# A FiLM layer on one core: x kept whole in SBUF as four slabs, longer transfer runs, small loads on another queue, rows split between VectorE and GpSimd

## The chip, the cores and the metric

One NeuronCore of a Trainium2 chip. The metric is device microseconds of that core, lower is better. Each figure is the median of a kernel's fast runs; runs of the kernel before, taken on the same chip in the same rounds, stand beside each. An execution counts as slow when it takes over 1.5% more than the fastest of the same kernel; slow ones are left out.

Names in the profiles: PE is TensorE (matmul), PEld its weight load, DVE VectorE, ACT ScalarE, POOL GpSimd, SP SyncE; a q behind a name stands for that engine's queue, with its waits and DMA issues. L100 is line 100 of the kernel. The profile counts 16 DMA engines for the core. A run is a stretch of contiguous bytes of one partition, and in the traces here each run of x or of the output is one packet (before: 4096 packets of 8 KB; after: 128 of 8, 1024 of 16, 128 of 24 and 384 of 32 KB). "Before" is the kernel before, "after" the changed one.

## The reference

```python
gamma = conditioning @ gamma_proj          # (32, 64) @ (64, 256)
beta = conditioning @ beta_proj
return x * (1 + gamma[:, None, :]) + beta[:, None, :]    # x: (32, 512, 256) float32
```

x is 16.8 MB, the output is as large, and all else is 0.14 MB.

## The kernel before

Two batch entries (1 MB) make a tile of 128 partitions with 8 rows of 256 in each. A small matmul spreads gamma and beta of the two entries over the partitions, into PSUM. VectorE does `(gamma + 1) * x` and `+ beta` in place. SyncE issues all loads, ScalarE all stores, 12 tiles are in flight.

```python
nc.sync.dma_start(out=cond_s, in_=conditioning)
nc.sync.dma_start(out=gbproj[:, :dim], in_=gamma_proj)
nc.sync.dma_start(out=gbproj[:, dim:], in_=beta_proj)
# ... cond_T, gb_s (32 x 512), one-hot matrix rident ...
for bg in range(0, batch, 2):                                   # 16 turns
    nc.sync.dma_start(out=x_tile, in_=...)                      # 1 MB, 8 KB per partition
    nc.tensor.matmul(gbbc, lhsT=onehot, rhs=gb_s, ...)          # 128 x 512 into PSUM
    nc.vector.scalar_tensor_tensor(out=x_tile, in0=gbc_k, scalar=1.0, in1=x_tile, op0=add, op1=mult)
    nc.vector.tensor_add(out=x_tile, in0=x_tile, in1=bbc_k)
    nc.scalar.dma_start(out=..., in_=x_tile)                    # 1 MB, 8 KB per partition
```

Of the kernel before, what the change touches and what calls it, by code (L numbers as in the profile page):

```python
# [2 lines left out]

# [5 lines left out]


@with_exitstack
def kernel(
    ctx: ExitStack,
    tc: tile.TileContext,
    x: bass.AP,
    conditioning: bass.AP,
    gamma_proj: bass.AP,
    beta_proj: bass.AP,
    out: bass.AP,  # L20
):
    nc = tc.nc
    f32 = mybir.dt.float32

    batch, seq, dim = x.shape
    cond_dim = conditioning.shape[1]
    assert conditioning.shape == (batch, cond_dim)
    assert gamma_proj.shape == (cond_dim, dim)
    assert beta_proj.shape == (cond_dim, dim)
    assert batch <= 128 and cond_dim <= 128  # L30

    P = 128
    assert seq % P == 0
    K = seq // P

    x_flat = x.flatten_outer_dims()
    out_flat = out.flatten_outer_dims()

    consts = ctx.enter_context(tc.tile_pool(name="consts", bufs=1))
    work = ctx.enter_context(tc.tile_pool(name="work", bufs=12))  # L40
    psum = ctx.enter_context(tc.tile_pool(name="psum", bufs=6, space=bass.MemoryType.PSUM))

    def x_src(b):
        r0 = b * seq
        return x_flat[r0 : r0 + seq, :].rearrange("(p k) d -> p k d", p=P)

    def out_dst(b):
        r0 = b * seq
        return out_flat[r0 : r0 + seq, :].rearrange("(p k) d -> p k d", p=P)

    cond_s = consts.tile([batch, cond_dim], f32)
    nc.sync.dma_start(out=cond_s, in_=conditioning)  # L52

    gbproj = consts.tile([cond_dim, 2 * dim], f32)
    nc.sync.dma_start(out=gbproj[:, :dim], in_=gamma_proj)  # L55
    nc.sync.dma_start(out=gbproj[:, dim:], in_=beta_proj)

    ident = consts.tile([P, P], f32)
    make_identity(nc, ident)

    with tc.tile_pool(name="psum0", bufs=1, space=bass.MemoryType.PSUM) as psum0:
        cond_T_p = psum0.tile([cond_dim, batch], f32)
        nc.tensor.matmul(cond_T_p, lhsT=cond_s, rhs=ident[:batch, :batch],  # L63
                         start=True, stop=True)
        cond_T = consts.tile([cond_dim, batch], f32)
        nc.vector.tensor_copy(out=cond_T, in_=cond_T_p)  # L66

        gb_p = psum0.tile([batch, 2 * dim], f32)
        nc.tensor.matmul(gb_p, lhsT=cond_T, rhs=gbproj, start=True, stop=True)  # L69
        gb_s = consts.tile([batch, 2 * dim], f32)  # L70
        nc.vector.tensor_copy(out=gb_s, in_=gb_p)  # L71

    BG = 2
    assert batch % BG == 0 and P % BG == 0
    PG = P // BG
    KK = (BG * seq) // P
    assert PG * KK == seq

    rident = consts.tile([batch, batch * PG], f32)
    nc.vector.tensor_copy(  # L80
        out=rident.rearrange("p (b g) -> p b g", g=PG),
        in_=ident[:batch, :batch].to_broadcast([batch, batch, PG]),
    )

    for bg in range(0, batch, BG):
        x_tile = work.tile([P, KK, dim], f32, name="x_tile")
        r0 = bg * seq
        nc.sync.dma_start(  # L88
            out=x_tile,
            in_=x_flat[r0 : r0 + BG * seq, :].rearrange("(p k) d -> p k d", p=P),  # L90
        )

        onehot = rident[:batch, bg * PG : bg * PG + P]
        gbbc = psum.tile([P, 2 * dim], f32)
        nc.tensor.matmul(gbbc, lhsT=onehot, rhs=gb_s, start=True, stop=True)  # L95

        gbc = gbbc[:, :dim]
        bbc = gbbc[:, dim:]
        gbc_k = bass.AP(tensor=gbc.tensor, offset=gbc.offset,
                        ap=[gbc.ap[0], [0, KK], gbc.ap[1]])  # L100
        bbc_k = bass.AP(tensor=bbc.tensor, offset=bbc.offset,
                        ap=[bbc.ap[0], [0, KK], bbc.ap[1]])

        nc.vector.scalar_tensor_tensor(  # L104
            out=x_tile,
            in0=gbc_k,
            scalar=1.0,
            in1=x_tile,
            op0=mybir.AluOpType.add,
            op1=mybir.AluOpType.mult,  # L110
        )
        nc.vector.tensor_add(out=x_tile, in0=x_tile, in1=bbc_k)  # L112

        nc.scalar.dma_start(
            out=out_flat[r0 : r0 + BG * seq, :].rearrange("(p k) d -> p k d", p=P),
            in_=x_tile,
        )


# [1 line left out]
_INS = ['x', 'conditioning', 'gamma_proj', 'beta_proj']  # L121
_OUTS = [((32, 512, 256), 'float32')]


# [23 lines left out]
```

## Time and profile before

| | before |
|---|---|
| time | 87.56 us (87.53 to 87.76) |
| span of the profiled execution | 85.5 us |
| moved by DMA | 33.70 MB, 4816 packets |
| VectorE busy | 72.5 us, 85% |
| GpSimd busy | 0.7 us |

The span runs from the first instruction to the last. In every run of this study but e6 the time is about 1.8 us more than its span (87.57 with 85.8, 84.35 with 82.6). A profile is one execution: the one shown here, with 85.5 us, is one of the faster ones. The prediction shows the strip of the transfers, the stretches, VectorE's two groups and the start; one view it left out is how long the small loads took from issue to landing (name, queue, how many, KB each, us):

```profile
gbproj<-in_gamma_proj_dram SPq DMA_DIRECT2D x1, 64.0 KB, 2.1
gbproj<-in_beta_proj_dram SPq DMA_DIRECT2D x1, 64.0 KB, 2.2
cond_s<-in_conditioning_dram SPq DMA_DIRECT2D x1, 8.0 KB, 1.5
```

Issued first, with nothing else to move, each lands within some 2 us. That will change.

### The profile page before, as it was taken

The page shows a single profiled execution, that of the slowest core. Times are in us where ns is not written, and L with a number is a line of the kernel's source. Part 1 is how long each engine was busy: PE and PEld are TensorE (multiplying, and loading weights), DVE is VectorE, ACT ScalarE, POOL GpSimd, SP SyncE. Part 2 cuts the span into 40 slices and gives each one's busy share as a digit, 9 for nine tenths or more (in the row PEclk, how much of TensorE's full clock was granted, in tenths as well). Part 3 has the DMA queues.
Part 4 walks back from the last instruction along what each step waited for, and adds up shares of the span by engine and source line. Part 5 has one row for each costly group of instructions (what it writes and reads, how often), then busy time and mean ns, then how long its engine had stood idle before and what let it go on. Part 6 is the DMA issues. An engine that isn't in the chain of part 4 may idle for free.

```text
span 85.5 us, 241 instructions
## 1 busy us (share of the span) xinstructions
PE 32.6 (38%) x36; PEld 9.6 (11%) x36; DVE 72.5 (85%) x35; POOL 0.7 (1%) x6
## 2 busy tenths in 40 slices
PE   0288999997059404950396019700000000000000
PEld 0203434340022002200220022000000000000000
DVE  3211899999999999999999999999999999999000
POOL 3000000000000000000000000000000000000000
DMA  0689999999999999999999999999999999999991
GB/s 4 123 368 418 425 429 425 429 330 356 429 429 425 429 429 429 429 429 425 429 425 429 429 429 429 418 429 429 429 425 429 429 425 429 418 429 422 429 429 58
DMA packets 4816, 33.70 MB, mean 394 GB/s; under 512 B 592, under 2 KB 720, under 8 KB 720
## 3 DMA queue, kind: packets, MB, share of 16 engines
q1 hardware_dynamic: 2512, 16.92, 48.9%
q10 hardware_dynamic: 2304, 16.78, 46.4%
HBM read 16.92 MB, written 16.78 MB: 394 GB/s over the span
## 4 chain that ended last, share of the span: by engine, by line
DMA 43%; DVE 32%; issue 9%; PE 5%; DVEq 3%; SPq 1%
DMA x_tile<-in_x_dram 28%; DVE x_tile L104 20%; DMA out_dram<-x_tile 12%; DVE x_tile L112 11%; DMA gbproj<-in_beta_proj_dram 3%; DVEq L143 3%; PE gbbc L95 2%; PE gb_p L69 2%; DVE gb_s L71 1%; SPq L55 1%; SPq L52 0%; SPq L88 0%; DVEq L104 0%
## 5 line engine op out<-in xcount | busy, mean ns | idle before, releaser
L104 DVE SCALAR_TENSOR_TENSOR x_tile<-gbbc,x_tile 128x2048 f32<-128x2048 f32 x16 | 35.9, 2283 | 2.2 <-PE gbbc L95 2.2
L95 PE MATMUL gbbc<-gb_s,rident 32*128 32x512 f32 x32 | 30.3, 1094 | 18.8 <-DVE x_tile L112 18.0
L112 DVE TENSOR_TENSOR x_tile<-x_tile,gbbc 128x2048 f32<-128x2048 f32 x16 | 35.8, 2279 | 0.0
L95 PEld LDWEIGHTS gbbc<-gb_s,rident 32*128 32x128 f32 x32 | 9.1, 317 | 40.2 <-issue 30.8
L71 DVE COPY gb_s<-gb_p 32x512 f32<-32x512 f32 x1 | 0.7, 679 | 3.1 <-PE gb_p L69 3.1
L69 PE MATMUL gb_p<-gbproj,cond_T 64*32 64x512 f32 x2 | 1.9, 1042 | 1.4 <-DMA gbproj<-in_beta_proj_dram 1.4
L80 DVE COPY rident<-ident 32x2048 f32<-32x2048 f32 x1 | 1.2, 1214 | 1.3 <-POOL ident masks.py:199 1.3
L63 PE MATMUL cond_T_p<-ident,cond_s 32*64 32x32 f32 x2 | 0.4, 284 | 2.4 <-DMA cond_s<-in_conditioning_dram 2.4
L63 PEld LDWEIGHTS cond_T_p<-ident,cond_s 32*64 32x64 f32 x2 | 0.3, 202 | 2.4 <-issue 2.4
L66 DVE COPY cond_T<-cond_T_p 64x32 f32<-64x32 f32 x1 | 0.2, 183 | 0.3 <-PE cond_T_p L63 0.3
L69 PEld LDWEIGHTS gb_p<-gbproj,cond_T 64*32 64x32 f32 x2 | 0.2, 132 | 1.5 <-issue 1.5
masks.py:199 POOL TENSOR_SCALAR_AFFINE_SELECT ident<-ident 128x128 f32<-128x128 f32 x1 | 0.3, 294 | 0.1
masks.py:197 POOL MEMSET ident<- 128x128 f32 x1 | 0.2, 205 | 0.3 <-POOLq L132 0.3
L132 POOL MEMSET const-bfloat16-1.0<- 128x1 bf16 x1 | 0.1, 102 | 0.0
L132 POOL MEMSET const-uint8-127<- 128x1 uint8 x1 | 0.1, 102 | 0.0
L132 POOL MEMSET const-float32-0.0<- 128x1 f32 x1 | 0.1, 99 | 0.2 <-issue 0.2
L132 POOL MEMSET const-float32-1.0<- 128x1 f32 x1 | 0.1, 99 | 0.0
## 6 DMA issues: line engine op xcount, KB each, us to landing
x_tile<-in_x_dram SPq DMA_DIRECT2D x16, 1024.0 KB, 20.5
out_dram<-x_tile ACTq DMA_DIRECT2D x16, 1024.0 KB, 12.4
gbproj<-in_gamma_proj_dram SPq DMA_DIRECT2D x1, 64.0 KB, 2.1
gbproj<-in_beta_proj_dram SPq DMA_DIRECT2D x1, 64.0 KB, 2.2
cond_s<-in_conditioning_dram SPq DMA_DIRECT2D x1, 8.0 KB, 1.5
```

What stands on the lines that cost most here:

```text
L55: nc.sync.dma_start(out=gbproj[:, :dim], in_=gamma_proj)
L63: nc.tensor.matmul(cond_T_p, lhsT=cond_s, rhs=ident[:batch, :batch], start=True, stop=True)
L66: nc.vector.tensor_copy(out=cond_T, in_=cond_T_p)
L69: nc.tensor.matmul(gb_p, lhsT=cond_T, rhs=gbproj, start=True, stop=True)
L71: nc.vector.tensor_copy(out=gb_s, in_=gb_p)
L80: nc.vector.tensor_copy(out=rident.rearrange("p (b g) -> p b g", g=PG), in_=ident[:batch, :batch].to_broadcast([batch, batch, PG]),)
L95: nc.tensor.matmul(gbbc, lhsT=onehot, rhs=gb_s, start=True, stop=True)
L104: nc.vector.scalar_tensor_tensor(out=x_tile, in0=gbc_k, scalar=1.0, in1=x_tile, op0=mybir.AluOpType.add, op1=mybir.AluOpType.mult,)
L112: nc.vector.tensor_add(out=x_tile, in0=x_tile, in1=bbc_k)
L132: nc = _bacc.Bacc("TRN2", target_bir_lowering=False, num_devices=1)
L143: with _tile.TileContext(nc) as tc:
```

## The change

The intent: all of x fits into SBUF (4 slabs of 32 KB per partition, 128 KB together, which the changed kernel holds), so no load ever has to wait for a buffer; the runs per partition grow from 8 KB to 32 KB (loads) and 16 KB (stores); x is issued at once while ScalarE's queue takes the small loads; GpSimd takes 5 of 16 rows from VectorE.

```diff
-    nc.sync.dma_start(out=cond_s, in_=conditioning)
+    nc.scalar.dma_start(out=cond_s, in_=conditioning)
...                                       # gamma_proj, beta_proj likewise
+    LOADS = {0: [8, 24]}                  # other slabs: one load of 32 rows
+    GROUP = 16
+    ON_DVE = 11
+    for s in range(SLABS):
+        xs = xpool.tile([P, ROWS, dim], f32, name=f"xs{s}")
+        for n in LOADS.get(s, [ROWS]):
+            nc.sync.dma_start(out=xs[:, r : r + n, :], in_=x_v[s, :, r : r + n, :])
...
+    for s in range(SLABS):                # gamma, beta of a slab: in PSUM, and in SBUF for GpSimd
+        nc.tensor.matmul(p_t, lhsT=cond_T[:, s * P : (s + 1) * P], rhs=gbproj, ...)
+        nc.scalar.activation(out=s_t[:, :dim], in_=p_t[:, :dim], func=Identity, bias=1.0, scale=1.0)
+        nc.scalar.copy(out=s_t[:, dim:], in_=p_t[:, dim:])
...
-        nc.vector.scalar_tensor_tensor(out=x_tile, ...)
-        nc.vector.tensor_add(out=x_tile, in0=x_tile, in1=bbc_k)
+        for r0 in range(0, ROWS, GROUP):
+            nc.vector.scalar_tensor_tensor(out=v, ...)            # 11 rows
+            nc.gpsimd.tensor_tensor(out=w, in0=w, in1=rows(g_s, nw), op=ALU.mult)   # 5 rows
+            nc.vector.tensor_add(out=v, ...)
+            nc.gpsimd.tensor_tensor(out=w, in0=w, in1=rows(b_s, nw), op=ALU.add)
+            nc.scalar.dma_start(out=o_v[s, :, r0 : r0 + GROUP, :], in_=xs[:, r0 : r0 + GROUP, :])
```

More of the change, by code (lines that the diff above doesn't have):

```diff
@@ L23 @@
     f32 = mybir.dt.float32
+    ALU = mybir.AluOpType
     batch, seq, dim = x.shape
     cond_dim = conditioning.shape[1]
-    assert conditioning.shape == (batch, cond_dim)
-    assert gamma_proj.shape == (cond_dim, dim)
-    assert beta_proj.shape == (cond_dim, dim)
-    assert batch <= 128 and cond_dim <= 128
     P = 128
-    assert seq % P == 0
-    K = seq // P
-    x_flat = x.flatten_outer_dims()
-    out_flat = out.flatten_outer_dims()
-    consts = ctx.enter_context(tc.tile_pool(name="consts", bufs=1))
@@ L40 @@
-    work = ctx.enter_context(tc.tile_pool(name="work", bufs=12))
-    psum = ctx.enter_context(tc.tile_pool(name="psum", bufs=6, space=bass.MemoryType.PSUM))
-    def x_src(b):
-        r0 = b * seq
-        return x_flat[r0 : r0 + seq, :].rearrange("(p k) d -> p k d", p=P)
-    def out_dst(b):
-        r0 = b * seq
-        return out_flat[r0 : r0 + seq, :].rearrange("(p k) d -> p k d", p=P)
+    SLABS = 4
+    BS = batch // SLABS
+    REP = P // BS
+    ROWS = BS * seq // P
+    assert SLABS * BS == batch and REP * BS == P and ROWS * REP == seq
@@ L51 @@
+    x_v = x.flatten_outer_dims().rearrange("(s p r) d -> s p r d", s=SLABS, p=P)
+    o_v = out.flatten_outer_dims().rearrange("(s p r) d -> s p r d", s=SLABS, p=P)
+    LOADS = {0: [8, 24]}
+    GROUP = 16
+    ON_DVE = 11
+    consts = ctx.enter_context(tc.tile_pool(name="consts", bufs=1))
+    xpool = ctx.enter_context(tc.tile_pool(name="xpool", bufs=1))
+    psum = ctx.enter_context(tc.tile_pool(name="psum", bufs=1, space=bass.MemoryType.PSUM))
     cond_s = consts.tile([batch, cond_dim], f32)
-    nc.sync.dma_start(out=cond_s, in_=conditioning)
+    nc.scalar.dma_start(out=cond_s, in_=conditioning)
@@ L54 @@
     gbproj = consts.tile([cond_dim, 2 * dim], f32)
-    nc.sync.dma_start(out=gbproj[:, :dim], in_=gamma_proj)
-    nc.sync.dma_start(out=gbproj[:, dim:], in_=beta_proj)
-    ident = consts.tile([P, P], f32)
-    make_identity(nc, ident)
-    with tc.tile_pool(name="psum0", bufs=1, space=bass.MemoryType.PSUM) as psum0:
-        cond_T_p = psum0.tile([cond_dim, batch], f32)
-        nc.tensor.matmul(cond_T_p, lhsT=cond_s, rhs=ident[:batch, :batch],
-                         start=True, stop=True)
-        cond_T = consts.tile([cond_dim, batch], f32)
-        nc.vector.tensor_copy(out=cond_T, in_=cond_T_p)
-        gb_p = psum0.tile([batch, 2 * dim], f32)
-        nc.tensor.matmul(gb_p, lhsT=cond_T, rhs=gbproj, start=True, stop=True)
-        gb_s = consts.tile([batch, 2 * dim], f32)
-        nc.vector.tensor_copy(out=gb_s, in_=gb_p)
@@ L73 @@
-    BG = 2
-    assert batch % BG == 0 and P % BG == 0
-    PG = P // BG
-    KK = (BG * seq) // P
-    assert PG * KK == seq
-    rident = consts.tile([batch, batch * PG], f32)
-    nc.vector.tensor_copy(
-        out=rident.rearrange("p (b g) -> p b g", g=PG),
-        in_=ident[:batch, :batch].to_broadcast([batch, batch, PG]),
-    )
-    for bg in range(0, batch, BG):
-        x_tile = work.tile([P, KK, dim], f32, name="x_tile")
-        r0 = bg * seq
-        nc.sync.dma_start(
-            out=x_tile,
-            in_=x_flat[r0 : r0 + BG * seq, :].rearrange("(p k) d -> p k d", p=P),
-        )
-        onehot = rident[:batch, bg * PG : bg * PG + P]
-        gbbc = psum.tile([P, 2 * dim], f32)
-        nc.tensor.matmul(gbbc, lhsT=onehot, rhs=gb_s, start=True, stop=True)
-        gbc = gbbc[:, :dim]
-        bbc = gbbc[:, dim:]
-        gbc_k = bass.AP(tensor=gbc.tensor, offset=gbc.offset,
-                        ap=[gbc.ap[0], [0, KK], gbc.ap[1]])
-        bbc_k = bass.AP(tensor=bbc.tensor, offset=bbc.offset,
-                        ap=[bbc.ap[0], [0, KK], bbc.ap[1]])
-        nc.vector.scalar_tensor_tensor(
-            out=x_tile,
-            in0=gbc_k,
-            scalar=1.0,
-            in1=x_tile,
-            op0=mybir.AluOpType.add,
-            op1=mybir.AluOpType.mult,
-        )
-        nc.vector.tensor_add(out=x_tile, in0=x_tile, in1=bbc_k)
-        nc.scalar.dma_start(
-            out=out_flat[r0 : r0 + BG * seq, :].rearrange("(p k) d -> p k d", p=P),
-            in_=x_tile,
-        )
@@ new lines @@
+    nc.scalar.dma_start(out=gbproj[:, :dim], in_=gamma_proj)
+    nc.scalar.dma_start(out=gbproj[:, dim:], in_=beta_proj)
+    slabs = []
+    for s in range(SLABS):
+        xs = xpool.tile([P, ROWS, dim], f32, name=f"xs{s}")
+        slabs.append(xs)
+        r = 0
+        for n in LOADS.get(s, [ROWS]):
+            nc.sync.dma_start(out=xs[:, r : r + n, :], in_=x_v[s, :, r : r + n, :])
+            r += n
+        assert r == ROWS
+    ident = consts.tile([batch, batch], f32)
+    make_identity(nc, ident)
@@ new lines @@
+    rident = consts.tile([batch, batch * REP], f32)
+    nc.vector.tensor_copy(
+        out=rident.rearrange("p (b g) -> p b g", g=REP),
+        in_=ident.to_broadcast([batch, batch, REP]),
+    )
+    cond_T_p = psum.tile([cond_dim, batch * REP], f32)
+    nc.tensor.matmul(cond_T_p, lhsT=cond_s, rhs=rident, start=True, stop=True)
+    cond_T = consts.tile([cond_dim, batch * REP], f32)
+    nc.vector.tensor_copy(out=cond_T, in_=cond_T_p)
+    gb_p, gb_s = [], []
+    for s in range(SLABS):
+        p_t = psum.tile([P, 2 * dim], f32, name=f"gb_p{s}")
+        nc.tensor.matmul(p_t, lhsT=cond_T[:, s * P : (s + 1) * P], rhs=gbproj,
+                         start=True, stop=True)
+        s_t = consts.tile([P, 2 * dim], f32, name=f"gb_s{s}")
+        nc.scalar.activation(out=s_t[:, :dim], in_=p_t[:, :dim],
+                             func=mybir.ActivationFunctionType.Identity,
+                             bias=1.0, scale=1.0)
+        nc.scalar.copy(out=s_t[:, dim:], in_=p_t[:, dim:])
+        gb_p.append(p_t)
+        gb_s.append(s_t)
@@ new lines, in rows @@
+    def rows(t, n):
+        return bass.AP(tensor=t.tensor, offset=t.offset, ap=[t.ap[0], [0, n], t.ap[1]])
+    for s in range(SLABS):
+        xs = slabs[s]
+        g_p, b_p = gb_p[s][:, :dim], gb_p[s][:, dim:]
+        g_s, b_s = gb_s[s][:, :dim], gb_s[s][:, dim:]
+        for r0 in range(0, ROWS, GROUP):
+            v = xs[:, r0 : r0 + ON_DVE, :]
+            w = xs[:, r0 + ON_DVE : r0 + GROUP, :]
+            nv, nw = ON_DVE, GROUP - ON_DVE
+            nc.vector.scalar_tensor_tensor(out=v, in0=rows(g_p, nv), scalar=1.0, in1=v,
+                                           op0=ALU.add, op1=ALU.mult)
+            nc.gpsimd.tensor_tensor(out=w, in0=w, in1=rows(g_s, nw), op=ALU.mult)
+            nc.vector.tensor_add(out=v, in0=v, in1=rows(b_p, nv))
+            nc.gpsimd.tensor_tensor(out=w, in0=w, in1=rows(b_s, nw), op=ALU.add)
+            nc.scalar.dma_start(out=o_v[s, :, r0 : r0 + GROUP, :],
+                                in_=xs[:, r0 : r0 + GROUP, :])
```

## The prediction

> **What bounds the kernel now.** I read the utilisation strip of the page first, because a kernel that reads 16.8 MB, does two operations per element and writes 16.8 MB is probably held by its transfers. The two rows are 40 slices of 2.14 us: busy share of the DMA engines in tenths, and what they moved.
>
> ```profile
> DMA  0689999999999999999999999999999999999991
> GB/s 4 123 368 418 425 429 425 429 330 356 429 429 425 429 429 429 429 429 425 429 425 429 429 429 429 418 429 429 429 425 429 429 425 429 418 429 422 429 429 58
> DMA packets 4816, 33.70 MB, mean 394 GB/s; under 512 B 592, under 2 KB 720, under 8 KB 720
> ```
>
> From slice 4 to slice 39 the engines are full, but for a dip in slices 9 and 10. 33.70 MB at 428 GB/s is 78.7 us of an 85.5 us span. So time can only be won at the start (some 4 us), in the dip, at the end, or by raising 428. The busy time by stretches confirms that nothing else is asked for (columns: stretch and length, PE, PEld, DVE, POOL busy, clock, DMA share, GB/s):
>
> ```profile
> 10.00:15.60 5.60, 5.60 (x8) 2.11 (x7) 5.60 (x4) 0.00 (x0) 1.00 1.01 426
> 15.60:20.00 4.40, 4.40 (x7) 1.54 (x5) 4.40 (x3) 0.00 (x0) 1.00 1.03 354
> 25.00:40.00 15.00, 7.67 (x8) 1.49 (x6) 15.00 (x8) 0.00 (x0) 1.00 1.01 428
> 60.00:79.00 19.00, 0.00 (x0) 0.00 (x0) 19.00 (x9) 0.00 (x0) 1.00 1.01 427
> 79.00:85.50 6.50, 0.00 (x0) 0.00 (x0) 0.32 (x1) 0.00 (x0) 1.00 0.73 306
> ```
>
> VectorE is full too (the groups of instructions say why: 32 instructions of 2.28 us, 71.7 us in all), so there are two nearly equal limits; but VectorE stops at 79.3 us and the last store still has to move after it. The chain that ended last mixes both.
>
> ```profile
> L104 DVE SCALAR_TENSOR_TENSOR x_tile<-gbbc,x_tile 128x2048 f32<-128x2048 f32 x16 | 35.9, 2283 | 2.2 <-PE gbbc L95 2.2
> L112 DVE TENSOR_TENSOR x_tile<-x_tile,gbbc 128x2048 f32<-128x2048 f32 x16 | 35.8, 2279 | 0.0
> ```
>
> Third, the start, in the time order of SyncE's issues (start, duration) and the first store:
>
> ```profile
> 0.73 0.38 SPq L52 DMA_DIRECT2D cond_s<-in_conditioning_dram  x1
> 1.18 0.53 SPq L55 DMA_DIRECT2D gbproj<-in_gamma_proj_dram  x1
> 1.75 0.58 SPq L56 DMA_DIRECT2D gbproj<-in_beta_proj_dram  x1
> 2.38 24.19 SPq L88 DMA_DIRECT2D x_tile<-in_x_dram  x12
> 15.61 11.33 ACTq L114 DMA_DIRECT2D out_dram<-x_tile  x4
> ```
>
> The three small loads hold SyncE for 1.65 us (2.38 - 0.73) before the first load of x is issued. In the single packet records of the trace the first x packet starts at 3.6 us, 1.2 us after its issue, and the last store packet ends at 84.1 us; the span closes 1.4 us later, and the measured 87.56 us is 2.06 us more than the span. I keep these last two as they are.
>
> The packet records give two more things. First, one packet took 15 to 18 ns for 256 B, 46 ns for 1024 B and 309 ns for 8192 B: a line of slope 0.0367 ns per byte and a fixed 8.4 ns. Successive packets of one engine overlap by 3 ns, so about 5 ns are lost per packet: 306 ns per 8 KB, 428 GB/s on 16 engines, as the strip says. Second, from 20 to 68 us each engine takes the load queue and the store queue strictly in turn, one 8 KB packet of each.
>
> [...]
>
> **The change part by part.**
>
> *Start.* The small loads move to ScalarE's queue and x is issued first. The first x issue goes from 2.38 to 0.73 us: 1.65 us earlier, the first packet at about 2.0 us. The small loads now share the engines: per engine 2 packets of 16 ns, 8 of 46 ns and some semaphore writes, 0.4 us; part of it falls into the first x packets' latency (they took 0.8 to 1.25 us instead of 0.31). I charge 0.3. Net 1.35 us won.
>
> *Runs.* Before, each engine moves 4096/16 = 256 x and out packets. After, a partition's run is 32 KB for slabs 1 to 3, 8 and 24 KB for slab 0: 5 loads of 128 packets are 40 per engine; 8 stores of 128 are 64. That is 104 instead of 256; 152 x 5 ns = 0.76 us won, plus 19 fewer semaphore writes per engine, which is nearly nothing. I count 0.7.
>
> *Compute.* VectorE's 2816 columns scale to 2.281 x 2816/2048 = 3.1 us, 16 of them 50 us instead of 72.[...] A group of 16 rows takes 6.2 us on VectorE[...]. This 22 us relief is off the path as long as the stores never run dry; the first group even comes later, because rows 0 to 10 need both loads of slab 0.
>
> *Does it stay off the path?* Slab 0 (4.19 MB) lands at about 2.0 + 0.6 + 9.8 + 0.4 = 12.8 us. The small loads alternate with x packets and beta_proj may come as late as 9 or 10 us; PE then needs 2.1 us per slab (two passes of 1.04 us), so gamma and beta are ready at about 12, no loss. First store issued at 19.5 us, moving at 20.7, where 7.6 MB of x are in. If the queues still alternate by packets, a load packet is 32 KB and a store packet 16 KB, so loads get two thirds, 286 GB/s. The remaining 9.2 MB take 32 us: x is complete at 53 us. By then VectorE has finished six groups (12.6 MB), of which 4.6 MB are stored; the last two groups are ready at 59.5 and 66 us, while the backlog of 8 MB alone keeps the engines busy until 71.5 us. No gap; the last store ends when 33.70 MB have moved.
>
> *Dip.* Between 17.5 and 20.3 us the packet records show load packets of 480 to 750 ns until the first store packet starts at 19.83, 4.2 us after its issue. About 1 us of transfer is lost. I see no reason why it should vanish, and keep it.
>
> *Sum.* 87.56 - 1.35 - 0.7 = 85.5 us, 2.35% less.
>
> **The rivals.**
>
> 1. Equal bytes for loads and stores (long runs are cut up and alternate in smaller pieces). Then the last 9.2 MB of x take 43 us and slab 3 lands at 63.8; its groups are ready at 70.3 and 76.5 us. The backlog (12.6 - 9.2 = 3.4 MB) ends at about 71.7, the next store at 76.6, and the last can move only at 77.7: a gap of about 1 us. Time 86.5. The strict turn of one run speaks against it; nothing in the trace has runs of two lengths in turn.
> 2. GpSimd is the bound. At 3.5 us[...], sixteen take 56 us, and with two thirds for loads this is still hidden (start at 13.5, done at 70). At over 4 us, 64 us of work end at 78 us and the last 2 MB store (4.9 us) ends at 84: about 87 to 88.[...]
> 3. The dip grows with the run. [...]the first store waits for longer packets, and 1 us lost becomes 2: 86.5 us.
> 4. The 5 ns are not per packet but per bytes moved (cut inside at some fixed size): the runs win nothing, 86.2 us. The line through 256 B, 1024 B and 8192 B speaks against it.
>
> **Range and chances.** The start is nearly certain (1.35 +- 0.3). Rivals 1, 3 and 4 each have a chance near one in five and each costs 0.7 to 1 us, and two of them together reach 87. Rival 2 has one in ten. Better than 84.6 would need the dip to go as well. 2% faster is 85.81 us, only 0.3 above my number, so faster gets 0.6, same 0.37, slower 0.03.
>
> **What would show it.** In the changed profile: first SyncE issue at 0.7 us and the strip full from slice 2; 16 GpSimd instructions[...] and 16 of VectorE near 3.1, neither stretched where they overlap; GB/s of 431 to 433 where loads or stores run; x complete near 53 us with the load queue at twice the store queue's bytes; VectorE done near 66 us with some 15 us of stores after it, and no hole in the last ten slices. x complete near 64 us means rival 1; a hole before the last store means rival 1 or 2; a dip over 2 us wide in bytes means rival 3. I am wrong altogether if the long runs lower the rate itself[...].

## The result, and the profile after

The changed kernel takes 84.54 us (84.35 to 84.64, 4 runs) against 87.62 us of the kernel before in the same rounds. The ratio is 0.9647, with a 95% interval of 0.9622 to 0.9672. A ratio here is always the mean time of one kernel's fast runs over that of the other's of the same rounds, so it isn't quite the ratio of the medians. The direction and the verdict (faster by over 2%) were right; the time lies 0.06 us under the predicted range and 0.96 us under the predicted number.

The strip of the transfers, as for the kernel before (a slice is now 2.06 us):

```profile
DMA  3899999969969989998889979899999999999992
GB/s 56 337 508 397 389 397 524 460 302 508 508 270 492 508 381 381 413 476 381 381 381 556 460 302 460 381 468 421 429 452 389 468 421 421 460 389 452 437 421 87
DMA packets 2080, 33.69 MB, mean 408 GB/s; under 512 B 288, under 2 KB 416, under 8 KB 416
```

The engines are at eight tenths in the second slice and full from the third, a slice earlier than before. The GB/s jump from 270 to 556 only because a packet of 32 KB is counted as a whole; nothing follows from one slice. 4816 packets have become 2080.

The start, in order of time:

```profile
0.74 9.89 SPq L59 DMA_DIRECT2D xs<-in_x_dram  x5
0.74 0.40 ACTq L48 DMA_DIRECT2D cond_s<-in_conditioning_dram  x1
1.17 0.51 ACTq L50 DMA_DIRECT2D gbproj<-in_gamma_proj_dram  x1
1.72 0.61 ACTq L51 DMA_DIRECT2D gbproj<-in_beta_proj_dram  x1
...
14.76 7.16 PE L79 MATMUL gb_p<-gbproj,cond_T 64*128 64x512 f32 x8 [8.90 <-DMA gbproj<-in_beta_proj_dram]
...
17.52 3.09 DVE L100 SCALAR_TENSOR_TENSOR xs<-gb_p,xs 128x2816 f32<-128x2816 f32 x1 [10.94 <-ACT gb_s L85]
...
25.94 4.32 ACTq L105 DMA_DIRECT2D out_dram<-xs  x2
```

x is issued at 0.74 us. But PE waits for beta until 14.76, VectorE starts at 17.52 instead of 8.89, and the first store goes out at 25.94 instead of 15.61. The small loads' issue-to-landing times say why:

```profile
gbproj<-in_gamma_proj_dram ACTq DMA_DIRECT2D x1, 64.0 KB, 9.1
gbproj<-in_beta_proj_dram ACTq DMA_DIRECT2D x1, 64.0 KB, 12.9
cond_s<-in_conditioning_dram ACTq DMA_DIRECT2D x1, 8.0 KB, 3.0
```

64 KB take 12.9 us: their packets wait their turn behind packets of x. In the packet records the 128 packets of 1 KB (46 to 54 ns each) start from 5.61 to 12.80 us, 112 of them just as a packet of x ends, and those of 24 KB took 912 to 1005 ns. The groups of instructions, with the mean ns of one:

```profile
L102 POOL TENSOR_TENSOR xs<-xs,gb_s 128x1280 f32<-128x1280 f32 x8 | 23.0, 2895 | 16.2 <-ACT gb_s L82 16.2
L100 DVE SCALAR_TENSOR_TENSOR xs<-gb_p,xs 128x2816 f32<-128x2816 f32 x8 | 24.7, 3083 | 10.9 <-ACT gb_s L85 10.9
L103 DVE TENSOR_TENSOR xs<-xs,gb_p 128x2816 f32<-128x2816 f32 x8 | 24.7, 3086 | 0.3
L104 POOL TENSOR_TENSOR xs<-xs,gb_s 128x1280 f32<-128x1280 f32 x8 | 23.0, 2893 | 0.0
```

VectorE now works for 49.4 us in 16 instructions and ends at 66.6 us. The chain that ended last is a trap here:

```profile
DVE 49%; DMA 16%; issue 11%; PE 2%; ACTq 1%; ACT 1%
```

It adds up to 80% and stops where VectorE does. The missing fifth is the 16 us in which the queued stores drain: nothing waits for them but the end of the program. The stretch from 67 to 80 us (columns as in the prediction, with ACT added before POOL) shows what really ends last:

```profile
67.00:80.00 13.00, 0.00 (x0) 0.00 (x0) 0.00 (x0) 0.00 (x0) 0.00 (x0) 1.00 1.01 435
```

No engine computes, the DMA engines are full. So a ledger of the transfers must hold the whole difference. I made one from the traces' packet records. "First x packet" is where it starts. "Packets' own" is what the packets of x and of the output need back to back: 0.0367 ns per byte and 5.4 ns per packet, by the prediction's line, summed and divided by 16 engines. The line was drawn through packets of up to 8 KB; in the changed kernel it holds for longer ones too: undisturbed packets of 16 KB took 611 ns and of 32 KB 1213 ns, where it gives 610 and 1211 (with the 3 ns of overlap). On 16 engines that is 431 and 433 GB/s, against 428 with 8 KB. "Lost" is the rest up to the end of the last packet. It includes the small loads' packets (an estimate by the same line: 0.37 us per engine) where these come after the first x packet, as in the changed kernel. "Closing" goes from there to the end of the span.

| us | first x packet | packets' own | lost | closing | span |
|---|---|---|---|---|---|
| before | 3.59 | 78.33 | 2.20 | 1.40 | 85.52 |
| after | 1.74 | 77.51 | 2.14 | 1.18 | 82.57 |
| difference | -1.85 | -0.82 | -0.06 | -0.22 | -2.95 |
| predicted | -1.65 | -0.7 | +0.3 | 0 | -2.05 |

### The profile page after: what moved, and what is told of

Read it like the earlier page. It is cut to its first block, busy times and chain, and to the rows that moved or that the text cites. A ratio compares the mean times of both kernels' runs of the same rounds, so it can differ in the third digit from the quotient of the medians.

```text
span 82.6 us, 156 instructions
## 1 busy us (share of the span) xinstructions
PE 9.1 (11%) x10; PEld 2.8 (3%) x10; DVE 49.9 (60%) x18; ACT 3.9 (5%) x9; POOL 46.2 (56%) x22
## 3 DMA queue, kind: packets, MB, share of 16 engines
q1 hardware_dynamic: 720, 16.78, 48.6%
## 4 chain that ended last, share of the span: by engine, by line
DVE 49%; DMA 16%; issue 11%; PE 2%; ACTq 1%; ACT 1%
DVE xs L100 30%; DVE xs L103 19%; DMA gbproj<-in_beta_proj_dram 16%; PE gb_p L79 2%; ACTq L50 1%; ACTq L48 0%; ACT gb_s L82 0%; ACT gb_s L85 0%
## 5 line engine op out<-in xcount | busy, mean ns | idle before, releaser
L102 POOL TENSOR_TENSOR xs<-xs,gb_s 128x1280 f32<-128x1280 f32 x8 | 23.0, 2895 | 16.2 <-ACT gb_s L82 16.2
L100 DVE SCALAR_TENSOR_TENSOR xs<-gb_p,xs 128x2816 f32<-128x2816 f32 x8 | 24.7, 3083 | 10.9 <-ACT gb_s L85 10.9
L103 DVE TENSOR_TENSOR xs<-xs,gb_p 128x2816 f32<-128x2816 f32 x8 | 24.7, 3086 | 0.3
L104 POOL TENSOR_TENSOR xs<-xs,gb_s 128x1280 f32<-128x1280 f32 x8 | 23.0, 2893 | 0.0
L79 PE MATMUL gb_p<-gbproj,cond_T 64*128 64x512 f32 x8 | 7.2, 1074 | 8.9 <-DMA gbproj<-in_beta_proj_dram 8.9
L74 DVE COPY cond_T<-cond_T_p 64x512 f32<-64x512 f32 x1 | 0.7, 683 | 4.3 <-PE cond_T_p L72 4.3
L79 PEld LDWEIGHTS gb_p<-gbproj,cond_T 64*128 64x128 f32 x8 | 2.5, 328 | 13.7 <-issue 13.7
L72 PE MATMUL cond_T_p<-rident,cond_s 32*64 32x512 f32 x2 | 1.9, 1065 | 3.9 <-DMA cond_s<-in_conditioning_dram 3.9
L82 ACT ACTIVATE gb_s<-gb_p 128x256 f32<-128x256 f32 x4 | 1.5, 383 | 16.4 <-PE gb_p L79 16.4
L85 ACT COPY gb_s<-gb_p 128x256 f32<-128x256 f32 x4 | 1.5, 367 | 0.0
## 6 DMA issues: line engine op xcount, KB each, us to landing
gbproj<-in_beta_proj_dram ACTq DMA_DIRECT2D x1, 64.0 KB, 12.9
```

The costliest lines, as they stand in the source:

```text
L72: nc.tensor.matmul(cond_T_p, lhsT=cond_s, rhs=rident, start=True, stop=True)
L74: nc.vector.tensor_copy(out=cond_T, in_=cond_T_p)
L79: nc.tensor.matmul(p_t, lhsT=cond_T[:, s * P : (s + 1) * P], rhs=gbproj, start=True, stop=True)
L82: nc.scalar.activation(out=s_t[:, :dim], in_=p_t[:, :dim], func=mybir.ActivationFunctionType.Identity, bias=1.0, scale=1.0)
L85: nc.scalar.copy(out=s_t[:, dim:], in_=p_t[:, dim:])
L100: nc.vector.scalar_tensor_tensor(out=v, in0=rows(g_p, nv), scalar=1.0, in1=v, op0=ALU.add, op1=ALU.mult)
```

## The experiments

Sixteen runs on several chips. Numbers like "0.9812" are ratios to the kernel before, with the 95% interval in brackets. The changed kernel repeats well (e12), so I compare with 84.54 to 84.68 us, ratio 0.9647 to 0.9663.

### e12, the changed kernel again

> The changed kernel once more, unchanged, on the chip of these runs: how far time and losses repeat. Expected 84.5 us, ratio to the kernel before 0.9647 within 0.003; x's first packet at 1.74 us, 0.3 to 0.6 us lost where the stores begin. A loss there of 0.8 us or more would say that it varies by itself.

84.68 us, 0.9663 (0.9646 to 0.9681). Ledger 1.73, 77.51, 2.47, 1.16. The terms repeat but for "lost", which differs by 0.33 us between two executions of one kernel: single profiles can't settle less than that. Against the kernel before, "lost" is here 0.27 us more, not 0.06 less. The part of it where the stores begin was 0.46 us in one and 0.58 in the other.

### e1, only the start undone

```diff
-    nc.scalar.dma_start(out=cond_s, in_=conditioning)
+    nc.sync.dma_start(out=cond_s, in_=conditioning)
...   # gamma_proj and beta_proj likewise
```

> The changed kernel with only the start undone: the three small loads back on SyncE's queue, ahead of x. Theory (the transfers set the end, and the start is worth what the trace says): the first x packet comes 1.85 us later (3.6 instead of 1.74 us), but the 0.69 us that x lost between 4 and 14 us to the small loads' packets come back: 84.54 + 1.85 - 0.69 = 85.7 us. Compute starts 3 us earlier (about 14 us), which must not change the end. Rival (the prediction's step, 1.35 us): 85.9. Rival (the late gamma and beta cost time): faster than 84.5.

86.04 us, 0.9812 (0.9787 to 0.9836). The start is worth 1.36 to 1.50 us here. The first x packet came at 3.61 us. VectorE started at 14.8 instead of 17.5 us, and that changed nothing for the better: the late gamma and beta cost no time, that rival falls. The packet records of the changed kernel agree: in no 4 us from 36 to 80 us does it lose more than 0.01 us, so the stores never ran dry. The expected 85.7 was 0.34 us too low. In its one profile 0.22 us more were lost where the stores begin (0.68 against 0.46), which is less than single profiles can settle.

### e2, only the runs undone

```diff
-    LOADS = {0: [8, 24]}
+    LOADS = {s: [8, 8, 8, 8] for s in range(4)}
-            nc.scalar.dma_start(out=o_v[s, :, r0 : r0 + GROUP, :], in_=xs[:, r0 : r0 + GROUP, :])
+            for q in range(r0, r0 + GROUP, 8):
+                nc.scalar.dma_start(out=o_v[s, :, q : q + 8, :], in_=xs[:, q : q + 8, :])
```

> The changed kernel with only the runs undone: 16 loads and 16 stores of 8 rows (8 KB per partition). Theory (about 5 ns lost per packet, 256 instead of 104 data packets per engine): 0.8 us more, 85.35 us, steady rate 428 instead of 431 to 433 GB/s; queues in equal shares, x complete near 65 us instead of 48.6, no gap before the last store. Rival 4 of the prediction (the loss goes with bytes): 84.5. Rival (the shorter dip, 0.46 us lost instead of 0.87, comes from the long runs): another 0.4 us, 85.75.

85.69 us, 0.9774 (0.9749 to 0.9799): the runs are worth 1.0 to 1.15 us, more than the 0.8 expected. Its ledger: 1.73, 78.33, 2.28, 1.48. Against the changed kernel 0.82 us are the packets' own, as the line through the packet sizes said, so the rival "the loss goes with bytes" falls; 0.3 us are in the closing stretch, of which later. The loss where the stores begin was 0.39 us, so long runs are not what made it small. The queues moved equal bytes (ratio 0.99 from 28 to 60 us) and x was complete at 63.6 us, with no gap.

### e3, only the loads' runs undone

```diff
-    LOADS = {0: [8, 24]}
+    LOADS = {s: [8, 8, 8, 8] for s in range(4)}
```

> Only the loads' runs are cut to 8 KB, the stores keep 16 KB. Theory (queues take turns packet by packet, whatever their length): loads now get one third instead of two thirds while stores are queued; x is complete only near 71 us, the stores starve for some 4 us in all, and the last group is ready near 78 us, so the last 2 MB move alone: 89 to 90 us, slower than either the long or the all-short runs. Rival (equal bytes for the queues, or the share doesn't matter): 85 us.

88.19 us, 1.0065 (1.0042 to 1.0087): 0.65% slower than the kernel before, and 2.5 us slower than with all runs short. The strip shows the hole:

```profile
GB/s 46 349 417 376 425 425 425 425 425 440 413 349 429 425 432 432 429 417 432 444 417 429 451 417 421 444 425 436 402 429 425 38 243 485 364 485 402 448 463 23
```

The 38 and 243 near 67 to 71 us are the DMA engines waiting for the last rows to be loaded and computed: x was complete only at 67.6 us and VectorE ended at 78.3. From 30 to 60 us the loads moved 4.29 MB and the stores 8.59 MB, 0.50 to 1. In the changed kernel it is 3.15 to 1.57 MB from 36.5 to 47.5 us, 2.00 to 1. So here the queues took turns run by run, and the longer run got the larger share. My simple reckoning said 89 to 90 us, x complete at 71; the direction and the hole were right, the size was 1 to 2 us too large.

### e4, GpSimd's rows back on VectorE

```diff
-    ON_DVE = 11
+    ON_DVE = 16
-            nc.gpsimd.tensor_tensor(...)          # both
```

> The changed kernel with all 16 rows of a group on VectorE, GpSimd idle. Theory: 16 instructions of 4.5 us, 72 us, starting at 17.5 us, end at 89.5; the last 2 MB store then moves alone for 4.9 us: span about 97, time 98 to 99 us. The relief of VectorE is off the path in the new kernel only because it has replaced what the late start of compute takes. Rival (VectorE was never the limit, 72 us fit into 82): 84.5 to 86.

96.47 us, 1.1003. One group and the strip of transfers:

```profile
L99 DVE SCALAR_TENSOR_TENSOR xs<-gb_p,xs 128x4096 f32<-128x4096 f32 x8 | 35.1, 4418 | 10.9 <-ACT gb_s L85 10.9
...
DMA  3998999999899899999979996999500299970792
```

VectorE works without a break from 17.7 to 87.3 us and the transfers have holes of some 7 and 3 us before the last two stores. The split of rows buys 12 us here, though it buys nothing in the kernel before (e6). 98 to 99 us were expected, from 4.5 us per instruction and 72 us in all; it was 4.42 and 69.6.

### e5, the start alone, on the kernel before

```diff
-    nc.sync.dma_start(out=cond_s, in_=conditioning)
+    nc.scalar.dma_start(out=cond_s, in_=conditioning)
...   # gamma_proj and beta_proj likewise, in the kernel before
```

> The kernel before with only the start changed: small loads on ScalarE's queue, x first. Theory: the first x packet comes at 1.74 instead of 3.59 us, but the small loads' 13 packets per engine now each wait for an 8 KB packet of x, so gamma and beta land at about 7.5 us instead of 4, VectorE's unbroken 71.7 us start at 12.3 instead of 8.9, end at 82.7 and the last 1 MB moves after them: span about 87.5, 89.5 us, slower than before. Rival (only transfers bound the kernel before): 1.2 to 1.8 us less than before, 86.

91.68 us, 1.0476 (1.0451 to 1.0500): the same edit that wins 1.4 us in the changed kernel loses 4.2 here. VectorE's first and last instructions, and the strip:

```profile
14.03 4.49 DVE L104 SCALAR_TENSOR_TENSOR x_tile<-gbbc,x_tile 128x2048 f32<-128x2048 f32 x2 [2.16 <-PE gbbc L95]
...
79.98 4.48 DVE L112 TENSOR_TENSOR x_tile<-x_tile,gbbc 128x2048 f32<-128x2048 f32 x2
```

```profile
DMA  3899999999999999999999999999999928920992
```

beta landed 7.4 us after its issue, VectorE started at 14.0 instead of 8.9 us and ended at 84.5 instead of 79.3. x did come at 1.75 us, but near the end the transfers had to wait for VectorE. Its start was 5.1 us later and the time grew by 4.2, so in the kernel before VectorE has only about 1 us to spare (an estimate). I expected 89.5 as I put beta's landing at 7.5 us; it was 9.1.

### e6, the split alone, on the kernel before

```diff
+        # ScalarE copies gamma + 1 and beta of this tile to SBUF
-        # 8 rows on VectorE
+        # 6 rows on VectorE, 2 on GpSimd (two tensor_tensor each)
```

> The kernel before with only the split of rows: 6 of 8 rows on VectorE, 2 on GpSimd, gamma and beta copied to SBUF by ScalarE for GpSimd. VectorE's busy time falls from 72 to about 55 us. Theory (transfers bound the kernel before): 87.6 us, within 0.3. Rival (VectorE, at 85 % of the span, is the bound or a joint one): 86 or less.

88.09 us, 1.0070 (1.0047 to 1.0093). VectorE's load fell and the transfers stayed full:

```profile
PE 31.6 (37%) x36; PEld 9.6 (11%) x36; DVE 55.8 (65%) x35; ACT 11.3 (13%) x33; POOL 40.7 (47%) x38
...
DMA  0499999999999999999999999999999999999990
```

16.7 us less on VectorE bought nothing: the kernel before is bound by its transfers. The time even grew by 0.6 us. Some 0.4 of that lies outside the span (time less span is 2.2 us in all five executions, 1.8 elsewhere), so the transfers didn't lose it; I didn't look for its cause.

### e9, start and runs both undone

```diff
    # the edits of e1 and e2 together
```

> The changed kernel with both the start and the runs undone: small loads first on SyncE's queue, 8 KB runs in 16 loads and 16 stores. What is left of the change is x resident in four slabs, gamma and beta per slab and the 11:5 split. Theory (the two parts add, undoing them cost 1.5 and 1.15 us, and the rest is worth next to nothing): 84.55 + 2.65 = 87.2 us, 0.4 us or less under the kernel before, with lost transfer time near 20 us back at 0.7 to 0.9 us. Rival (residency or the split is worth something of its own, where the parts overlap): 86.6 or less.

87.37 us, 0.9975 (0.9961 to 0.9989). What remains of the change, residency and split, is worth 0.24 us by itself. And the two parts nearly add: starting from e9, long runs alone (that is e1) win 1.33 us and the early start alone (e2) 1.68 us; on top of the other part each wins some 0.3 us less (1.0 to 1.15 and 1.36 to 1.50).

### e7 and e16, one queue for loads and stores

```diff
-            nc.scalar.dma_start(out=o_v[s, :, r0 : r0 + GROUP, :], ...)
+            nc.sync.dma_start(out=o_v[s, :, r0 : r0 + GROUP, :], ...)
```

> The changed kernel with its stores issued by SyncE, on the queue of the loads and so behind them[...]: no load and store are in turn, x is complete near 41 us, stores follow. It asks what the loss of 0.46 us at 28 to 34 us (0.87 at 16 to 22 us in the kernel before) belongs to. If it belongs to two queues starting to take turns, it goes: 84.0 us. If it belongs to the first writes to HBM after reads, it stays, only later: 84.5. If the change from reads to writes empties the engines: 85 or more.

84.55 us, 0.9655 (0.9634 to 0.9675), two of six executions and the profile in the slow state, so its packet records tell nothing about the question. Hence once more:

> The kernel of e7 once more, for a profile in the fast state. If the loss where stores begin belongs to two queues starting to take turns, no stretch of 4 us after 30 us loses more than 0.15 us; if it belongs to the first writes after reads, 0.3 us or more are lost near 41 us. Time 84.5 us either way, as e7's fast runs had it.

84.56 us, 0.9665 (0.9643 to 0.9687), profile in the fast state. Now loads and stores are never in turn, and still 0.62 us are lost from 40 to 44 us, where the loads end and the first stores begin. So here the loss came with the first writes after reads, without queues starting to take turns.

### e10, the store queue used early

```diff
+    warm = consts.tile([batch, cond_dim], f32)
+    nc.scalar.dma_start(out=warm, in_=conditioning)      # in the kernel before
```

> The kernel before with one addition: ScalarE's queue gets an 8 KB load (conditioning once more, into a tile that nobody reads) at the very start, so that the first store is not the first use of that queue. The loss where the stores begin was 0.87, 0.93 and 0.68 us in the three kernels whose small loads went on SyncE's queue, and 0.31 to 0.64 in the six with them on ScalarE's. Theory (the greater loss goes with the first use of the queue): the loss falls to about 0.5 us and the time by 0.3 to 0.4, 87.2 us. Rival (it goes with something else that the start changes, or differs from execution to execution): 0.8 to 0.9 us lost as before, 87.55 us.

87.52 us, 0.9991 (0.9979 to 1.0002), and 0.86 us lost where the stores begin. My theory that the larger loss is the queue's first use falls.

### e8, one store per slab

```diff
-            nc.scalar.dma_start(out=o_v[s, :, r0 : r0 + GROUP, :], ...)    # per group
+        nc.scalar.dma_start(out=o_v[s], in_=xs)                             # per slab
```

> A try for a better version: one 4 MB store per slab, 32 KB per partition, instead of two. Theory (5 ns per packet): 32 fewer packets per engine, 0.17 us less, 84.35 us; the first store starts 6 us later, the last slab is still ready (67 us) long before the queue empties, queues in equal shares, x complete near 52 us. Rival (longer runs lengthen the dip): 84.9 or more.

84.64 us, 0.9676 (0.9653 to 0.9700): no gain. The packets' own time fell by 0.17 us to 77.33 as expected, but the closing stretch was 1.43 us instead of 1.18.

### e11, small loads behind the first load of x

```diff
     nc.sync.dma_start(out=xs[:, 0:8, :], ...)
+    nc.sync.dma_start(out=cond_s, in_=conditioning)       # and gamma_proj, beta_proj
     nc.sync.dma_start(out=xs[:, 8:32, :], ...)
```

> A try for a better version: the small loads on SyncE's queue behind the first 1 MB load of x, so that x starts first and yet no small packet takes turns with a packet of x. Theory (0.69 us were lost at 4 to 14 us to the turns, against some 0.45 us that the small packets take by themselves): 84.3 us, gamma and beta landing near 6 us and compute starting near 13. Rival (the loss is the small packets' own, or the first use of ScalarE's queue by the stores costs 0.3 us again): 84.5 to 84.8.

84.77 us, 0.9689 (0.9657 to 0.9720): no gain. From 4 to 8 us 0.89 us were lost, more than the 0.69 of the changed kernel from 4 to 14 us. In both some 0.36 us are the small packets' own, wherever they stand. (The profiled execution was a slower one, span 83.8 us.)

### e13, e14 and e15, the closing stretch

The records of SyncE's semaphore instructions show what it does at the end: waits, mostly for two semaphores per instruction, 62 ns apart. In the kernel before four come after the last landing (84.52, 84.58, 84.64 and 84.70 us), in the changed kernel one (81.76), in e8 five and in e2 and e9 six, with closing stretches of 1.43, 1.48 and 1.50 us. In the traces of the kernel before and the changed one the DMAs use eight semaphores in turn (35 in the kernel before, 4 or 5 on each; 16 in the changed one, 2 on each), so the last store's place in the row of waits should follow from the number of DMAs. Three kernels add only 256-byte loads that nobody reads:

```diff
+    pad0 = consts.tile([1, cond_dim], f32)
+    nc.scalar.dma_start(out=pad0, in_=conditioning[0:1, :])
```

One of them in the changed kernel:

> The changed kernel with one more DMA, 256 bytes into a tile that nobody reads, on ScalarE's queue at the start: 17 DMAs instead of 16. Theory (the eight DMA semaphores are used in turn, SyncE waits for them in a fixed order at the end, and the last store's place in that order is the number of DMAs modulo 8): the last store now sits first in the order, seven more waits of 62 ns follow its landing: the stretch from the last packet to the end of the span goes from 1.18 to about 1.6 us, the time from 84.6 to 85.05 us. Rival (the stretch goes with the length of the last packets): 1.18 us and 84.6 to 84.7.

84.70 us, 0.9680 (0.9663 to 0.9697). Three waits after the landing instead of one, the closing stretch 1.33 us instead of 1.18. The count moved it, in the expected direction, but by a third of what I reckoned: I had counted one wait per semaphore and the order of their use, not of their numbers.

Five of them in the kernel before:

> The kernel before with five such 256-byte loads: 40 DMAs instead of 35. Theory: the last store is last in the order of the waits; the stretch from the last packet to the end goes from 1.40 to 1.17 us, the time from 87.6 to 87.35. Rival (the stretch goes with the length of the last packets): no change, 87.6 or a little more.

87.31 us, 0.9978 (0.9965 to 0.9991): one wait after the landing, closing stretch 1.19 us, 0.2 us faster by nothing but five useless loads. The rival, that the stretch goes with the length of the last packets, falls: these are of 8 KB.

Four of them with e8's stores:

> A try for a better version: one 4 MB store per slab as in e8, with four 256-byte loads so that there are 16 DMAs again. Theory: e8 gained 0.17 us by longer runs and lost 0.25 us at the end; with the end mended 84.35 us, 0.2 to 0.3 under e8's 84.64. Rival (the 256-byte loads in turn with x packets cost as much again, or the later loads now wait for them): 84.6 or more.

85.05 us, 0.9716 (0.9699 to 0.9733). The closing stretch is 1.17 us as wanted, but the later loads now wait for the landings of the loads whose semaphores they reuse: the second load of x is issued at 4.0 instead of 1.16 us. More is lost: 0.88 us from 4 to 8 us, 0.77 where the stores begin. (In the changed kernel the fifth load waits so for gamma_proj, 7.6 us, but other loads of x fill its queue meanwhile.) No better version was found; the changed kernel stays the best.

## Why the prediction was right or wrong

**The bound: right.** Transfers set the end in both kernels. e6 takes 17 us off VectorE for nothing, and the changed kernel drains its stores for 16 us with all engines idle.

**First x packet: mis-sized, 1.65 predicted, 1.85 measured.** From the issue at 0.73 us I took the 1.2 us from issue to first packet of a load that was fourth on its queue. As the first on its queue it took 1.0 us (0.74 to 1.74), as the small load in that place did before (0.73 to 1.74).

**"I charge 0.3" and "keep" the dip: the step that failed, the largest miss of the ledger.** The prediction let "lost" grow by 0.3 us. In the profiles it fell by 0.06 us (e12: grew by 0.27). The medians settle it better: the time fell by 3.08 us, in e12 by 2.93, and the three terms that repeat make 2.9 of it (1.85, 0.82 and 0.22 to 0.24), so "lost" fell by some 0.0 to 0.2 us (an estimate). The small loads' turns cost more than charged, 0.69 us from 4 to 14 us, about half of it their packets' own. What made up for that is the dip, which I saw no reason to change: 0.46 us in the changed kernel, 0.58 in e12, instead of 0.87. In the two profiles the first packets' slow start was also 0.16 us cheaper, and the engines ended closer together (0.14 us less lost after 80 us). Why the dip shrank stays open, see below.

**Start as a whole: near, partly by luck.** e1 against the changed kernel gives 1.36 to 1.50 us, e9 against e2, with short runs, 1.68; I said 1.35. The parts were further off and cancelled: x moved 0.2 us earlier than predicted, the turns cost 0.39 more, and the dip is 0.2 us (e1) to 0.4 us (e9, before) smaller with the early start.

**Runs: mechanism right, size too low, the largest miss by the experiments.** 0.82 us of packets' own time against 0.76 worked out and 0.7 counted. The semaphore writes that I put at nearly nothing are packets of 4 bytes and 9 ns in both traces, 561 before and 257 after: 19 fewer per engine, 0.17 us at most (an estimate), which the ledger has under "lost". In time the runs won 1.0 to 1.3 us (e2, and e9 against e1), because 0.3 us of the closing stretch went with the number of DMAs, which the longer runs changed. Residency and split, which I counted as nothing, add 0.24 us (e9).

**"I keep these last two as they are": wrong for one of them.** The stretch after the last packet went from 1.40 to 1.18 us; e13 and e14 show it to be a matter of how many waits follow the last landing. What lies outside the span is the same in both kernels, but 1.8 us and not 2.06: I had set the median time against the span of a faster execution.

The sum: 0.2 + 0.36 + 0.12 + 0.22 = 0.90 us is what the four terms missed from span to span, all in one direction (the 0.36 is no surer than the 0.33 by which two profiles of one kernel differ). The remaining 0.13 us between this and the medians (3.08 against 2.95) is the difference of single executions.

**Compute off the path: right, with more slack lost than I thought.** gamma and beta came at 14.6 us, not 9 or 10, so compute began at 17.5 and not near 13, and the first store at 25.9 instead of 19.5. The end didn't move, as e1 shows. With compute 8.6 us later than in the kernel before, the relief by GpSimd became necessary (e4), and without it the start alone is a loss (e5). Even from 13 us on, e4's 69.6 us of VectorE would have ended at 82.6, after the changed kernel's last packet (81.4; an estimate). That coupling I hadn't predicted: I had called the relief merely off the path.

**Rivals.** Rival 1 (equal bytes) is out: 2.00, 0.50 and 0.99 to 1 with runs of 32:16, 8:16 and 8:8 KB. x was complete at 48.6 us instead of 53, since the stores started later. Rival 2 is out, though nothing measured had spoken against it (the trace before has GpSimd busy for 0.7 us, in no instruction of this kind): a GpSimd instruction took 2.89 us, and VectorE's 3.08 us is what its own times in e4 and before give for 2816 columns (4.42 us for 4096 and 2.28 for 2048: 2.28 + 768 x 2.14/2048 = 3.08). GpSimd took 2.88 us in e2 and e3 for an instruction beside which VectorE was all but idle (at 47.7 and 54.2 us). So neither was stretched noticeably. Rival 3 (the loss grows with the run) is out: 0.39 us with short runs, 0.31 with 32 KB stores. Rival 4 is out by the ledger of e2 and the durations of 16 and 32 KB packets.

**Open:** what sets the loss where stores begin. It was 0.68 to 0.93 us in the kernels whose first transfers are the small loads alone (before, e1, e6, e9, e10, and 0.80 in e14) and mostly 0.31 to 0.64 in those that start with x (0.77 in e15). It is no matter of the queue's first use (e10), of two queues in turn (e16) or of run length (e2). No run tells why, and it is worth 0.4 us at most.

## What to carry to other kernels

When transfers are full from start to end, make a ledger: when the first packet moves, what the packets need by themselves, what is lost between, and what follows the last. Here two queues shared by run and not by byte (2.00, 0.50 and 0.99 to 1 for runs of 32:16, 8:16 and 8:8 KB), so try the longer run on the queue whose data others wait for; and 64 KB that shared the engines with long runs landed very late (12.9 us, against 2.2 us by themselves). A change of one part can be a loss alone (e5, e3) and a gain beside the part that makes room for it, so test parts both alone and taken out.
